# Keys and values turned in 32x32 blocks by VectorE and moved to their rows by DMAs, and another order of the steps of a head

## The chip, the core and the metric

The kernel runs on one core of a Trainium2 chip. A core has five engines with instruction streams of their own: TensorE (PE, matmuls, with the loading of its weights as PEld), VectorE (DVE), ScalarE (ACT), GpSimd (POOL) and SyncE (SP, which here only issues DMAs). Engines wait for each other by semaphores. The metric is the device time of one execution in microseconds (us); lower is better.

## The reference

One inference step of a decoder of two layers: layer 0 mixes tokens by gated linear attention (GLA) with four heads, layer 1 by a gated MLP; each is followed by a dense MLP. There are 256 prompt tokens and 8 x 8 sample tokens, 320 columns in all, and a carried state for each of the 8 sample sequences and 4 heads. The change is in the GLA layer:

```python
def step(s, inp):
    qi, ki, vi, gi = inp
    b = jnp.cumsum(gi, axis=-2)
    b_last = b[..., -1:, :]
    q_dec = qi * jnp.exp(b)
    k_inv = ki * jnp.exp(-b)
    k_to_end = ki * jnp.exp(b_last - b)
    scores = jnp.where(causal, jnp.einsum('bhtk,bhsk->bhts', q_dec, k_inv), 0.0)
    o = (jnp.einsum('bhtk,bhkv->bhtv', q_dec, s)
         + jnp.einsum('bhts,bhsv->bhtv', scores, vi))
    s_new = (jnp.exp(b_last[..., 0, :])[..., None] * s
             + jnp.einsum('bhsk,bhsv->bhkv', k_to_end, vi))
    return s_new, o
...
o = o * lax.rsqrt(jnp.mean(jnp.square(o), axis=-1, keepdims=True) + HEAD_NORM_EPS) * norm_g
o = o.reshape(bsz, t, GLA_VAL_DIM).astype(x.dtype) * jax.nn.silu(r)
return o @ w_out, s_fin.astype(s0.dtype)
```

A head has 256 key columns and 512 value columns; its state is 256 x 512. The last two einsums sum over tokens (s), so they want keys and values with tokens along the partitions, while the projections leave them with features along the partitions.

## The kernel before

**Weight products.** Activations are held as features x 320 tokens. Every weight product is three matmuls of a high and a low part (mm3, lines 161 to 163). A unit is 512 KB of weights: SP loads it into raw (line 138, three buffers), ACT casts it to wh (line 144), DVE subtracts to wl (line 145), and PE runs 24 matmuls on it, into PSUM tiles mm (four banks). The bulk of the kernel is this stream.

**A head.** Each head projects its keys and queries (project_kq), values (project_v) and gates r (project_r), in the order v, kq, r for head 0 and kq, v, r for the others. When a product is done, ev_k, ev_q and ev_v evict it. ev_k makes kend (keys decayed to the end, prompt) and kst (sample keys as high and low parts); PE transposes both (lines 420 and 422, with ident as the other operand) into a PSUM tile gl, from where ACT copies the prompt part to ktp (424) and ACT and DVE in turn copy 32 rows each into kz (429, 431). ev_v copies the prompt values to vfm (447), makes vst, transposes both on PE (456, 458), and copies them to vtp (ACT, 460) and vts (DVE, 461). Over four heads these are 96 transposes of 128x128.

**The steps of a head.** While PE runs the next projection, a Side object puts a head's attention in between, some steps after each unit. The steps are sample_scores, sample_first (loads of states 0 and 1 by SP, line 578, and the first part of the sample output hd.po, line 587), and then sixteen sample steps (sequence b, half kt), with prompt_scores, prompt_o(0), prompt_o(1), prompt_state(0) and prompt_state(1) one after every two of them. A sample step takes the high and low part of the state (ACT sth, line 597; DVE stl, line 598), adds two matmuls to hd.po (line 600), forms the update kz x vts on PE (line 603), and DVE decays and adds it to the state (line 604); after the second half POOL writes the state (line 607). Step (b, 0) loads the state of sequence b + 2. prompt_o multiplies scores and vtp (lines 542, 543; ACT copies and squares, DVE sums), prompt_state ktp and vtp (line 558; ACT copies to S, line 560; POOL writes it, line 562). Last come sample_o (copy, four transposes, sum, square, reduction, a product with ones, and a reciprocal root by ACT and DVE, lines 612 to 625 and 186 to 190), weigh (506) and finish (512).

**What sets the order.** The engines' instruction order is fixed when the program is built: a scheduler places the instructions of the steps and of the weight stream by its own estimate of when they are ready. PSUM tiles gl have four buffers; the tiles with tag st (states, S, and at the start xr) have four too; kz, qm and scst are single. The steps of the last head lie beside the product with w_out (first group mm of its first columns, over four quarters q of its rows, of which the last needs head 3's output). second_half flushes the remaining steps, closes the heads' pools, opens new ones and loads z with POOL.

Of the kernel before, what the change touches and what calls it, by code (L numbers as in the profile page):

```python
# [8 lines left out]
F32 = mybir.dt.float32  # L9
F32R = mybir.dt.float32r  # L10
# [67 lines left out]
def step_kernel(ctx: ExitStack, tc: tile.TileContext, A):  # L78
# [3 lines left out]
    def nm(s):  # L82
        uid[0] += 1
        return f"{s}_{uid[0]}"
# [198 lines left out]
    kz = gp.tile([P, 2, 4, DK], F32R, tag="kz", name="kz")  # L283
# [7 lines left out]
    def load_gates():  # L291

        nc.sync.dma_start(wgr, A["gla_w_low"])
        wgr2 = gp.tile([P, 2, DV], F32, tag="vtp", name="wgr2")[:].rearrange("p a b -> p (a b)")
# [32 lines left out]

    def chunks(ap):
        return ap.rearrange("p (n w) -> p n w", w=CH)

    class Head:
# [6 lines left out]
        def tiles(hd):  # L338
# [59 lines left out]

        def ev_k(hd, kt, ps):
# [17 lines left out]
            pt = gltile()  # L417
            ks = kst[:].rearrange("p b c t -> p (b c t)")
            for blk in range(2):
                nc.tensor.transpose(pt[:, blk * P : (blk + 1) * P], kend[:, blk * P : (blk + 1) * P], ident[:])  # L420
            for g in range(2):
                nc.tensor.transpose(pt[:, TP + g * P : TP + (g + 1) * P], ks[:, g * P : (g + 1) * P], ident[:])
            cs = slice(kt * P, (kt + 1) * P)
            nc.scalar.copy(hd.ktp[:, :, cs], pt[:, 0:TP].rearrange("p (b f) -> p b f", f=P))
            for i in range(4):
                rows = slice(32 * i, 32 * (i + 1))
                src = pt[rows, TP:].rearrange("p (b f) -> p b f", f=P)
                if i % 2:
                    nc.scalar.copy(kz[rows, :, i, cs], src)
                else:  # L430
                    nc.vector.tensor_copy(kz[rows, :, i, cs], src)
# [13 lines left out]
        def ev_v(hd, vt, ps):  # L445
            vfm = g2.tile([P, TP], F32, tag="vfm", name=nm("vfm"))
            nc.scalar.copy(vfm[:], ps[:, 0:TP])
# [5 lines left out]
            pt = gltile()  # L453
            vs = vst[:].rearrange("p b c t -> p (b c t)")
            for blk in range(2):
                nc.tensor.transpose(pt[:, blk * P : (blk + 1) * P], vfm[:, blk * P : (blk + 1) * P], ident[:])  # L456
            for g in range(2):
                nc.tensor.transpose(pt[:, TP + g * P : TP + (g + 1) * P], vs[:, g * P : (g + 1) * P], ident[:])  # L458
            cs = slice(vt * P, (vt + 1) * P)
            nc.scalar.copy(hd.vtp[:, :, cs], pt[:, 0:TP].rearrange("p (b f) -> p b f", f=P))  # L460
            nc.vector.tensor_copy(hd.vts[:, :, cs], pt[:, TP:].rearrange("p (b f) -> p b f", f=P))
# [71 lines left out]
        def prompt_o(hd, i):  # L533
# [19 lines left out]
        def prompt_state(hd, kt):  # L553
# [3 lines left out]
            for blk in range(2):  # L557
                nc.tensor.matmul(pu[:], hd.ktp[:, blk, kt * P : (kt + 1) * P], hd.vtp[:, blk, :],  # L558
                                 start=(blk == 0), stop=(blk == 1))
# [4 lines left out]
        def sample_scores(hd):  # L564
            for g in range(2):
# [14 lines left out]
        def sample_first(hd):  # L580

            hd.st = {}
            hd.load(0)
            hd.load(1)
# [520 lines left out]
```

## Time and profile before

| | us |
|---|---|
| median of three runs (2703.96 to 2704.41) | 2704.05 |
| the profiled execution's own time | 2703.75 |
| its span in the trace | 2702.0 |
| granted TensorE clock, mean | 0.999 |

The page of a profile has the busy time of each engine, the span in 40 slices, and the chain of work that ended last. A group of instructions is a line with its engine and operation, output<-input, the count, the summed busy time, the mean duration of one in ns, and the idle time of the engine just before them with what ended it. Matmuls overlap on PE, so their spacing in a timeline, not their duration, is what they take from it. In a timeline a row is a start, a length (of a run of equal instructions, with their count), and in brackets the idle time before it and what ended that. DMA rows show a queue, a size and the median time from issue to landing. The lines themselves stand in the prediction.

### The profile page before, as it was taken

How to read it: one execution, taken by the hardware profiler on the slowest of the kernel's cores; microseconds unless marked ns; L12 is line 12 of the kernel's file. 1: busy time of each engine (PE TensorE's matmuls, PEld its weight loads, DVE VectorE, ACT ScalarE, POOL GpSimd, SP SyncE). 2: the span in 40 equal slices, each digit the busy share in tenths (PEclk: the TensorE clock that was granted, in tenths of full speed). 3: DMA queues.
4: the chain of work that ended last, by engine and by line, in shares of the span. 5: the costliest groups of instructions: out<-in, count | busy, mean ns of one | idle time of the engine just before them, and what ended most of it. 6: DMA issues, size and time to landing. Idle time of an engine off the chain costs nothing.

```text
span 2702.0 us, 44679 instructions
## 1 busy us (share of the span) xinstructions
PE 2692.4 (100%) x18515; PEld 2669.7 (99%) x18515; DVE 1543.5 (57%) x2289; ACT 1182.8 (44%) x1702; POOL 53.5 (2%) x83
## 2 busy tenths in 40 slices
PE   9999999999999999999999999999999999999998
PEld 9999999999999999999999999999999999999998
DVE  6667577885444444444468775587444444444456
ACT  6545455464234334333445554355334323333434
POOL 1000001000000000000001000000000000000000
PEclk9999999999999999999999999999999999999999
DMA  7656556644445455444445444454444545554442
GB/s 243 193 188 228 185 190 218 211 146 156 152 151 154 151 154 151 153 151 153 150 148 171 150 140 136 140 162 155 150 155 150 154 151 153 152 153 152 153 152 79
DMA packets 126396, 434.53 MB, mean 161 GB/s; under 512 B 13680, under 2 KB 17904, under 8 KB 126192
## 3 DMA queue, kind: packets, MB, share of 16 engines
q1 hardware_dynamic: 119136, 407.82, 48.6%
q0 software_dynamic: 6512, 23.20, 2.6%
q8 instruction: 145, 2.38, 0.4%
q10 hardware_dynamic: 544, 0.66, 0.1%
q14 instruction: 59, 0.48, 0.1%
HBM read 409.60 MB, written 22.02 MB: 160 GB/s over the span
## 4 chain that ended last, share of the span: by engine, by line
PE 99%; ACT 0%; DMA 0%; DVE 0%; issue 0%; ACTq 0%; DVEq 0%
PE mm L161 32%; PE mm L163 31%; PE mm L162 31%; PE gl L600 1%; PE gl L603 1%; PE gl L558 1%; PE gl L948 0%; PE gl L542 0%; DMA raw<-gla_w_in 0%; ACT z L1038 0%; PE gl L943 0%; DMA xr<-xT 0%; PE gl L543 0%; PE gl L458 0%; PE gl L456 0%; PE gl L521 0%
## 5 line engine op out<-in xcount | busy, mean ns | idle before, releaser
L145 DVE TENSOR_TENSOR wl<-raw,wh 128x1024 fp32r<-128x1024 f32 (+1 forms) x740 | 901.6, 1219 | 938.8 <-ACT wh L144 936.3
L144 ACT CAST wh<-raw 128x1024 fp32r<-128x1024 f32 (+1 forms) x740 | 771.3, 1044 | 1201.3 <-PE mm L163 1080.9
L163 PE MATMUL mm<-yh,wh 128*128 128x320 f32 x2624 | 805.0, 307 | 0.0
L161 PE MATMUL mm<-yh,wl 128*128 128x320 f32 x2624 | 803.1, 308 | 0.0
L162 PE MATMUL mm<-yl,wh 128*128 128x320 f32 x2624 | 794.2, 303 | 0.0
L161 PE MATMUL mm<-hh,wl 128*128 128x320 f32 x2048 | 630.8, 308 | 0.0
L163 PE MATMUL mm<-hh,wh 128*128 128x320 f32 x2048 | 628.7, 307 | 0.0
L162 PE MATMUL mm<-hl,wh 128*128 128x320 f32 x2048 | 619.6, 303 | 0.0
L162 PEld LDWEIGHTS mm<-yl,wh 128*128 128x128 f32 x2624 | 492.5, 188 | 0.0
L161 PEld LDWEIGHTS mm<-yh,wl 128*128 128x128 f32 x2624 | 490.9, 188 | 0.0
L163 PEld LDWEIGHTS mm<-yh,wh 128*128 128x128 f32 x2624 | 490.8, 187 | 0.0
L162 PEld LDWEIGHTS mm<-hl,wh 128*128 128x128 f32 x2048 | 384.4, 188 | 0.0
L161 PEld LDWEIGHTS mm<-hh,wl 128*128 128x128 f32 x2048 | 384.4, 188 | 0.0
L163 PEld LDWEIGHTS mm<-hh,wh 128*128 128x128 f32 x2048 | 383.0, 187 | 0.0
L161 PE MATMUL mm<-xh,wl 128*128 128x320 f32 x768 | 241.1, 314 | 0.9 <-DVE wl L145 0.5
L163 PE MATMUL mm<-xh,wh 128*128 128x320 f32 x768 | 236.7, 308 | 0.0
L162 PE MATMUL mm<-xl,wh 128*128 128x320 f32 x768 | 234.7, 306 | 0.0
L161 PEld LDWEIGHTS mm<-xh,wl 128*128 128x128 f32 x768 | 144.1, 188 | 5.4 <-issue 1.9
L162 PEld LDWEIGHTS mm<-xl,wh 128*128 128x128 f32 x768 | 144.3, 188 | 3.5 <-issue 1.2
L163 PEld LDWEIGHTS mm<-xh,wh 128*128 128x128 f32 x768 | 143.9, 187 | 1.3
L857 DVE TENSOR_TENSOR hl<-f,hh 128x320 fp32r<-128x320 f32 x128 | 62.3, 489 | 29.4 <-ACT hh L856 29.4
L161 PE MATMUL mm<-oh,wl 128*128 128x320 f32 x256 | 78.1, 309 | 0.6 <-DVE nw L187 0.6
(268 smaller groups left out, 2112.2 us busy)
## 6 DMA issues: line engine op xcount, KB each, us to landing
raw<-mlp_w SPq DMA_DIRECT2D x512, 512.0 KB, 3.5
raw<-gla_w_in SPq DMA_DIRECT2D x94, 512.0 KB, 4.2
raw<-sg_w_in SPq DMA_DIRECT2D x64, 512.0 KB, 3.5
st<-state SPq DMA_DIRECT2D x32, 512.0 KB, 4.3
o_state_s<-st POOLq DMA_DIRECT2D x32, 512.0 KB, 3.8
raw<-gla_w_out SPq DMA_DIRECT2D x32, 512.0 KB, 4.2
raw<-sg_w_out SPq DMA_DIRECT2D x32, 512.0 KB, 3.5
z<-xT POOLq DMA_DIRECT2D x2, 1280.0 KB, 11.6
```

What stands on the lines that cost most here:

```text
L144: nc.scalar.copy(hi[:, ks, :], raw[:, ks, :])
L145: nc.vector.tensor_sub(lo[:, ks, :], raw[:, ks, :], hi[:, ks, :].bitcast(F32))
L161: nc.tensor.matmul(ps, wl[:, kk, s], x_h, start=first, stop=False)
L162: nc.tensor.matmul(ps, wh[:, kk, s], x_l, start=False, stop=False)
L163: nc.tensor.matmul(ps, wh[:, kk, s], x_h, start=False, stop=last)
L558: nc.tensor.matmul(pu[:], hd.ktp[:, blk, kt * P : (kt + 1) * P], hd.vtp[:, blk, :], start=(blk == 0), stop=(blk == 1))
L600: nc.tensor.matmul(po[:], qm[:, kt, b * P : (b + 1) * P], part[:], start=False, stop=(b == DB - 1 and kt == 1 and part is sth))
L603: nc.tensor.matmul(pu[:], kz[:, g, i, kt * P : (kt + 1) * P], hd.vts[:, g, :], start=True, stop=True)
L857: nc.vector.tensor_sub(hl[:, j, 0:T], f[:], hh[:, j, 0:T].bitcast(F32))
```

## The change

The transposes on PE and the copies behind them are dropped. DVE transposes the same 128x256 pieces in blocks of 32x32 (values straight from PSUM, keys from kend and kst) into a new tile blk, which is taken from the ring of tag st. A block is then turned in itself but stands in the wrong 32 partitions; gather moves the blocks to their rows by four DMAs (one for each source group i) of 32 partitions, with pieces of 128 bytes, for each target group q. Per head there are 32 such DMAs for the keys (POOL) and 32 for the values, of which eight (last half, odd q) go to ACT's queue and the rest to POOL. vtp and vts become one tile va, kz and ktp get another layout, and the readers take views of them. sample_scores and prompt_scores come first, then two empty steps (four in head 3), then sample_first, and the prompt parts stand ahead of sample steps 0, 2, 6 and 8. The loads of states 0 and 1 move into sample_scores.

```diff
--- before.py
+++ after.py
@@ -341,9 +345,18 @@
             hd.kip = gp.tile([P, 2, TP], F32, tag="kip", name=nm("kip"))
             hd.kte = gp.tile([P, 2, T], F32, tag="kte", name=nm("kte"))
             hd.kis = gp.tile([P, 2, DB, 4, DS], F32, tag="kis", name=nm("kis"))
-            hd.ktp = gp.tile([P, 2, DK], F32, tag="ktp", name=nm("ktp"))
-            hd.vtp = gp.tile([P, 2, DV], F32, tag="vtp", name=nm("vtp"))
-            hd.vts = gp.tile([P, 2, DV], F32R, tag="vts", name=nm("vts"))
+
+            hd.ktp = gp.tile([P, 2, 2, P], F32, tag="ktp", name=nm("ktp"))
+            hd.va = gp.tile([P, 2, 2, 2, 2, P], F32, tag="vtp", name=nm("va"))
+
+        def vt_prompt(hd, vt, blk):
+            return hd.va[:, vt // 2, 0, vt % 2, blk, :]
+
+        def v_prompt(hd, blk):
+            return hd.va[:, :, 0, :, blk, :]
+
+        def v_sample(hd, g):
+            return hd.va[:, :, 1, :, g, :].bitcast(F32R)
 
         def gate_logits(hd):
 
@@ -395,6 +408,18 @@
             nc.vector.tensor_copy(fac[:, :, 7:8], d3)
             nc.vector.tensor_mul(fac[:, :, 6:7], d2, d3)
             nc.vector.tensor_mul(fac[:, :, 5:6], fac[:, :, 2:3], d3)
+
+        def blocks(hd):
+
+            return g3.tile([P, 4, TP], F32, tag="st", name=nm("blk"))
+
+        def gather(hd, dst, blk, q, queue):
+
+            n = blk.shape[1] // P
+            src = blk.rearrange("p (n q f) -> p n q f", q=4, f=32)
+            out = dst.rearrange("p (n i f) -> p n i f", i=4, f=32)
+            for i in range(4):
+                queue.dma_start(out[32 * q : 32 * (q + 1), :, i, :], src[32 * i : 32 * (i + 1), :, q, :])
 
         def ev_k(hd, kt, ps):
             ei, ee = hd.ei[kt], hd.ee[kt]
@@ -414,21 +439,16 @@
             hi = kst[:, :, 0:2, :]
             nc.scalar.copy(hi.bitcast(F32R), bc4(kte[:, TP:T]).to_broadcast(two))
             nc.vector.tensor_sub(kst[:, :, 2:4, :], bc4(kte[:, TP:T]).to_broadcast(two), hi)
-            pt = gltile()
-            ks = kst[:].rearrange("p b c t -> p (b c t)")
-            for blk in range(2):
-                nc.tensor.transpose(pt[:, blk * P : (blk + 1) * P], kend[:, blk * P : (blk + 1) * P], ident[:])
-            for g in range(2):
-                nc.tensor.transpose(pt[:, TP + g * P : TP + (g + 1) * P], ks[:, g * P : (g + 1) * P], ident[:])
-            cs = slice(kt * P, (kt + 1) * P)
-            nc.scalar.copy(hd.ktp[:, :, cs], pt[:, 0:TP].rearrange("p (b f) -> p b f", f=P))
-            for i in range(4):
-                rows = slice(32 * i, 32 * (i + 1))
-                src = pt[rows, TP:].rearrange("p (b f) -> p b f", f=P)
-                if i % 2:
-                    nc.scalar.copy(kz[rows, :, i, cs], src)
-                else:
-                    nc.vector.tensor_copy(kz[rows, :, i, cs], src)
+            if kt == 0:
+                hd.kb = hd.blocks()
+            nc.vector.transpose(hd.kb[:, kt, :], kend[:])
+            nc.vector.transpose(hd.kb[:, 2 + kt, :], kst[:].rearrange("p b c t -> p (b c t)"))
+            if kt == 1:
+                kb = hd.kb[:].rearrange("p a b -> p (a b)")
+                for q in range(4):
+                    hd.gather(kz[:, q].bitcast(F32).rearrange("p k b f -> p (k b f)"), kb[:, 2 * TP :], q, nc.gpsimd)
+                for q in range(4):
+                    hd.gather(hd.ktp[:].rearrange("p k b f -> p (k b f)"), kb[:, 0 : 2 * TP], q, nc.gpsimd)
 
         def ev_q(hd, kt, ps):
             qd = hd.qd[:, kt, :]
@@ -443,22 +463,20 @@
             nc.vector.tensor_sub(qv[:, :, DB * DS : DB * DS + DS], qs, qv[:, :, 0:DS].bitcast(F32))
 
         def ev_v(hd, vt, ps):
-            vfm = g2.tile([P, TP], F32, tag="vfm", name=nm("vfm"))
-            nc.scalar.copy(vfm[:], ps[:, 0:TP])
+            if vt % 2 == 0:
+                hd.vb = hd.blocks()
+            nc.vector.transpose(hd.vb[:, vt % 2, :], ps[:, 0:TP])
             vst = g2.tile([P, DB, 4, DS], F32, tag="vst", name=nm("vst"))
             two = [P, DB, 2, DS]
             hi = vst[:, :, 0::2, :]
             nc.scalar.copy(hi.bitcast(F32R), bc4(ps[:, TP:T]).to_broadcast(two))
             nc.vector.tensor_sub(vst[:, :, 1::2, :], bc4(ps[:, TP:T]).to_broadcast(two), hi)
-            pt = gltile()
-            vs = vst[:].rearrange("p b c t -> p (b c t)")
-            for blk in range(2):
-                nc.tensor.transpose(pt[:, blk * P : (blk + 1) * P], vfm[:, blk * P : (blk + 1) * P], ident[:])
-            for g in range(2):
-                nc.tensor.transpose(pt[:, TP + g * P : TP + (g + 1) * P], vs[:, g * P : (g + 1) * P], ident[:])
-            cs = slice(vt * P, (vt + 1) * P)
-            nc.scalar.copy(hd.vtp[:, :, cs], pt[:, 0:TP].rearrange("p (b f) -> p b f", f=P))
-            nc.vector.tensor_copy(hd.vts[:, :, cs], pt[:, TP:].rearrange("p (b f) -> p b f", f=P))
+            nc.vector.transpose(hd.vb[:, 2 + vt % 2, :], vst[:].rearrange("p b c t -> p (b c t)"))
+            if vt % 2:
+                for q in range(4):
+                    hd.gather(hd.va[:, vt // 2].rearrange("p c v b f -> p (c v b f)"),
+                              hd.vb[:].rearrange("p a b -> p (a b)"), q,
+                              nc.scalar if vt == 3 and q % 2 else nc.gpsimd)
 
         def project_kq(hd, side):
 
@@ -538,9 +556,9 @@
             po = gltile()
             pv = po[:].rearrange("p (v t) -> p v t", t=TP)
             for v in range(2):
-                vs = slice((2 * i + v) * P, (2 * i + v + 1) * P)
-                nc.tensor.matmul(pv[:, v, :], hd.vtp[:, 0, vs], scp[:, 0:W0], start=(v == 0), stop=False)
-                nc.tensor.matmul(pv[:, v, P:TP], hd.vtp[:, 1, vs], scp[:, W0:], start=False, stop=(v == 1))
+                vt = 2 * i + v
+                nc.tensor.matmul(pv[:, v, :], hd.vt_prompt(vt, 0), scp[:, 0:W0], start=(v == 0), stop=False)
+                nc.tensor.matmul(pv[:, v, P:TP], hd.vt_prompt(vt, 1), scp[:, W0:], start=False, stop=(v == 1))
             nc.scalar.copy(o_all[:, 4 * h + 2 * i : 4 * h + 2 * i + 2, 0:TP], pv)
             sq = gp.tile([P, 2, TP], F32, tag="sq", name=nm("sq"))
             nc.scalar.activation(sq[:], pv, AF.Square)
@@ -555,13 +573,16 @@
                 hd.S = g3.tile([P, 2, DV], F32, tag="st", name=nm("S"))
             pu = gltile()
             for blk in range(2):
-                nc.tensor.matmul(pu[:], hd.ktp[:, blk, kt * P : (kt + 1) * P], hd.vtp[:, blk, :],
+                nc.tensor.matmul(pairs(pu), hd.ktp[:, kt, blk, :], hd.v_prompt(blk),
                                  start=(blk == 0), stop=(blk == 1))
             nc.scalar.copy(hd.S[:, kt, :], pu[:])
             if kt == 1:
                 nc.gpsimd.dma_start(A["o_state_p"][hd.h].rearrange("(k p) v -> p k v", p=P), hd.S[:])
 
         def sample_scores(hd):
+            hd.st = {}
+            hd.load(0)
+            hd.load(1)
             for g in range(2):
                 pc = gltile(32)
                 for kt in range(2):
@@ -579,12 +600,9 @@
 
         def sample_first(hd):
 
-            hd.st = {}
-            hd.load(0)
-            hd.load(1)
             hd.po = gltile()
             for g in range(2):
-                nc.tensor.matmul(hd.po[:], scst[:, g, :], hd.vts[:, g, :], start=(g == 0), stop=False)
+                nc.tensor.matmul(pairs(hd.po), scst[:, g, :], hd.v_sample(g), start=(g == 0), stop=False)
 
         def sample_step(hd, b, kt):
 
@@ -600,7 +618,7 @@
                 nc.tensor.matmul(po[:], qm[:, kt, b * P : (b + 1) * P], part[:], start=False,
                                  stop=(b == DB - 1 and kt == 1 and part is sth))
             pu = gltile()
-            nc.tensor.matmul(pu[:], kz[:, g, i, kt * P : (kt + 1) * P], hd.vts[:, g, :], start=True, stop=True)
+            nc.tensor.matmul(pairs(pu), kz[:, i, kt, g, :], hd.v_sample(g), start=True, stop=True)
             nc.vector.scalar_tensor_tensor(st[:, kt, :], st[:, kt, :], hd.dec[:, kt, NCH + b : NCH + b + 1],
                                            pu[:], op0=ALU.mult, op1=ALU.add)
             if kt == 1:
@@ -629,14 +647,17 @@
         def steps(hd):
 
             yield hd.sample_scores
+            yield hd.prompt_scores
+            for _ in range(2 if hd.h < H - 1 else 4):
+                yield lambda: None
             yield hd.sample_first
             sample = [lambda b=b, kt=kt: hd.sample_step(b, kt) for b in range(DB) for kt in range(2)]
-            prompt = [hd.prompt_scores, lambda: hd.prompt_o(0), lambda: hd.prompt_o(1),
-                      lambda: hd.prompt_state(0), lambda: hd.prompt_state(1)]
-            for i, p in enumerate(prompt):
-                yield p
-                yield from sample[2 * i : 2 * i + 2]
-            yield from sample[2 * len(prompt) :]
+            prompt = {0: lambda: hd.prompt_o(0), 2: lambda: hd.prompt_o(1),
+                      6: lambda: hd.prompt_state(0), 8: lambda: hd.prompt_state(1)}
+            for i, x in enumerate(sample):
+                if i in prompt:
+                    yield prompt[i]
+                yield x
             yield hd.sample_o
             yield hd.weigh
             yield hd.finish
```

The new order of the instructions is shown at two places. The names are tiles with the number of their buffer's use: st a state, sth and stl its high and low part, va the transposed values, gl and mm PSUM tiles, oh and ol the parts of the heads' output; line numbers are those of the file that the rows belong to.

First place, PE in the sample phase of head 3. Before, a piece of it near prompt_state (L600 the state's part of the output, L603 the update):

```order
L603 MATMUL gl_4555<-vts_3987,kz 128x512
L603 MATMUL gl_4564<-vts_3987,kz 128x512
L161 MATMUL mm_4577<-xh_89,wl_4581 128x320
L600 MATMUL gl_4374<-stl_4550,qm 128x512
L600 MATMUL gl_4374<-sth_4549,qm 128x512
L162 MATMUL mm_4577<-xl_90,wh_4580 128x320
L163 MATMUL mm_4577<-xh_89,wh_4580 128x320
L600 MATMUL gl_4374<-stl_4559,qm 128x512
L600 MATMUL gl_4374<-sth_4558,qm 128x512
L161 MATMUL mm_4577<-xh_89,wl_4581 128x320
```

Now, the start of the sample phase of head 3 on PE (L605 is sample_first, L560 and L561 are prompt_o, L618 and L621 the successors of L600 and L603):

```order
L161 MATMUL mm_4873<-oh_4868,wl_5109 128x320
L162 MATMUL mm_4873<-ol_4869,wh_5108 128x320
L605 MATMUL gl_4540<-va_4052,scst 128x512 x2
L560 MATMUL gl_4544<-scp,va_4052 128x256
L561 MATMUL gl_4544<-scp,va_4052 128x128
L560 MATMUL gl_4544<-scp,va_4052 128x256
L561 MATMUL gl_4544<-scp,va_4052 128x128
L618 MATMUL gl_4540<-stl_4556,qm 128x512
L618 MATMUL gl_4540<-sth_4555,qm 128x512
L621 MATMUL gl_4561<-va_4052,kz 128x512
L618 MATMUL gl_4540<-stl_4595,qm 128x512
L618 MATMUL gl_4540<-sth_4594,qm 128x512
```

And its end (L633 transposes the sample output, L643 is the product with ones):

```order
L618 MATMUL gl_4540<-stl_4932,qm 128x512
L618 MATMUL gl_4540<-sth_4931,qm 128x512
L633 MATMUL gl_4973<-ident,os_4971 128x128 x4
L643 MATMUL gl_4983<-s_694_4543,ones 128x320
L161 MATMUL mm_5246<-oh_4868,wl_5250 128x320
```

Before, weight matmuls stand between any few rows of the sample phase. Now the phase stands together: from L605 to L643 one weight matmul is left, the last of mm_4873; 143 of the products with w_out (mm_4870 to mm_4873, with parts oh and ol of heads 0 to 2) have moved ahead of it, and the next one, mm_5246, reads the weights wl_5250.

Second place, POOL's queue in head 0, ahead of and at the first state writes. Before:

```order
L262 AFFINE_SELECT ms_115<-ms_115 128x32
L262 AFFINE_SELECT ms_119<-ms_119 128x32
L607 DMA o_state_s<-st_926 128x2x512
L607 DMA o_state_s<-st_928 128x2x512
L607 DMA o_state_s<-st_981 128x2x512
L607 DMA o_state_s<-st_1072 128x2x512
```

Now (L422 is a gather, L625 the successor of L607):

```order
L262 AFFINE_SELECT ms_115<-ms_115 128x32
L262 AFFINE_SELECT ms_119<-ms_119 128x32
L422 DMA va_512<-blk_513 32x8x32 x16
L422 DMA va_512<-blk_540 32x8x32 x8
L422 DMA ktp_511<-blk_849 32x4x32 x6
L422 DMA kz<-blk_849 32x4x32 x16
L422 DMA ktp_511<-blk_849 32x4x32 x10
L625 DMA o_state_s<-st_936 128x2x512
```

Ahead of the first state write of head 0 stand 56 gathers where none stood.

More of the change, by code (lines that the diff above doesn't have):

```diff
@@ L280, in step_kernel @@
     nc.vector.memset(fac[:], 1.0)
[L283 removed]
+    kz = gp.tile([P, 4, 2, 2, P], F32R, tag="kz", name="kz")
     nc.gpsimd.memset(kz[:].bitcast(F32), 0.0)
@@ L293, in load_gates @@
         nc.sync.dma_start(wgr, A["gla_w_low"])
-        wgr2 = gp.tile([P, 2, DV], F32, tag="vtp", name="wgr2")[:].rearrange("p a b -> p (a b)")
+        wgr2 = gp.tile([P, 4, DV], F32, tag="vtp", name="wgr2")[:].rearrange("p a b -> p (a b)")[:, 0 : H * DK]
         for i in range(6):
```

2 lines of the change are left out of this document (added).

## The prediction

> **What bounds the kernel now.** I read the page first: its busy times, its chain of waits and the clock row.
>
> ```profile
> span 2702.0 us, 44679 instructions
> PE 2692.4 (100%) x18515; PEld 2669.7 (99%) x18515; DVE 1543.5 (57%) x2289; ACT 1182.8 (44%) x1702; POOL 53.5 (2%) x83
> ...
> PEclk9999999999999999999999999999999999999999
> ...
> PE 99%; ACT 0%; DMA 0%; DVE 0%; issue 0%; ACTq 0%; DVEq 0%
> ```
>
> TensorE (PE) is busy all the span at a full clock, and 99% of the chain that ends last is PE following PE. So two things alone move the time: PE work that goes away, and stretches in which PE has to stand. VectorE (DVE, 57%), ScalarE (ACT) and GpSimd (POOL, 2%) have room on average; what decides is whether they have it where PE waits for them.
>
> **What goes.** The groups of PE instructions by line give the transposes:
>
> ```profile
> L456 PE MATMUL gl<-ident,vfm 128*128 128x128 f32 x32 | 6.2, 271 | 0.0
> L458 PE MATMUL gl<-ident,vst 128*128 128x128 f32 x32 | 6.1, 272 | 0.0
> ...
> L422 PE MATMUL gl<-ident,kst 128*128 128x128 f32 x16 | 3.1, 272 | 0.0
> L420 PE MATMUL gl<-ident,kend 128*128 128x128 f32 x16 | 3.0, 271 | 0.0
> ```
>
> That is 96 instructions and 18.4 us busy. Matmuls overlap, so 18.4 us is an upper bound; the time they take from PE is their spacing, which PE's timeline in head 0 shows:
>
> ```profile
> 41.09 0.38 PE L456 MATMUL gl<-ident,vfm 128*128 128x128 f32 x2
> 41.31 0.38 PE L458 MATMUL gl<-ident,vst 128*128 128x128 f32 x2
> 41.53 0.38 PE L456 MATMUL gl<-ident,vfm 128*128 128x128 f32 x2
> 41.74 0.38 PE L458 MATMUL gl<-ident,vst 128*128 128x128 f32 x2
> 41.88 0.39 PE L161 MATMUL mm<-xh,wl 128*128 128x320 f32 x1
> 42.12 0.31 PE L162 MATMUL mm<-xl,wh 128*128 128x320 f32 x1
> 42.26 0.31 PE L163 MATMUL mm<-xh,wh 128*128 128x320 f32 x1
> ```
>
> Weight matmuls follow each other at 0.14. L162 starts at 42.12, so L161 behind eight transposes held PE from about 41.98: eight took 41.98 - 41.09 = 0.89 us, 0.111 each. 96 x 0.111 = **10.7 us less PE work**. This is also nearly all that can be gained, 0.40%: no other PE instruction leaves.
>
> **What comes on DVE, ACT and POOL.** Per head DVE gets 12 transposes of 128x256 and loses four casts of vts and four of kz; ACT loses fourteen copies.
>
> ```profile
> L447 ACT COPY vfm<-mm 128x256 f32<-128x256 f32 x16 | 6.0, 376 | 10.7 <-PE mm L163 10.7
> L461 DVE CAST vts<-gl 128x256 fp32r<-128x256 f32 x16 | 6.8, 423 | 7.9 <-ACT vtp L460 7.9
> L431 DVE CAST kz<-gl 32x256 fp32r<-32x256 f32 x16 | 6.6, 413 | 0.7 <-ACT ktp L424 0.4
> ```
>
> No row shows a DVE transpose. A pass over 128x256 took 0.42 us here (L461), a two-operand pass over 128x512 0.69; I take 0.42, so 12 x 0.42 - 4 x 0.42 - 4 x 0.41 = 1.7 us more DVE per head, from 0 to 5 by the two rows. That is off PE's path as long as DVE has idle time, and DVE's fullest stretch, the later steps of head 1, has little (columns: PE, weight loads, DVE, ACT, POOL busy with their counts, clock, DMA share, GB/s; the first row is head 3's later steps):
>
> ```profile
> 425.00:452.00 27.00, 27.00 (x165) 24.95 (x164) 21.89 (x34) 15.45 (x29) 4.13 (x6) 1.00 0.71 236
> 240.00:266.00 26.00, 26.00 (x177) 25.35 (x176) 24.71 (x48) 14.15 (x24) 1.45 (x2) 1.00 0.77 274
> ```
>
> 24.7 us of 26 (second row), with PE still busy all of it. The transposes themselves fall into the projections ahead of the steps; I put them at nothing, and keep 0 to 3 us of stalls for heads 0 to 2, of which I take 1, for steps that now run into the next head's projections.
>
> Per head the gathers are 56 DMAs on POOL and 8 on ACT. No row shows one of this kind (32 partitions, 4 or 8 pieces of 128 bytes). POOL's own rows bound the issue:
>
> ```profile
> L607 POOL DMA_DIRECT2D o_state_s<-st x32 | 23.3, 727 | 402.2 <-DVE st L604 391.5 <-DVE fac L393 10.7
> L909 POOL DMA_DIRECT2D bsp<-sg_wT x8 | 4.5, 573 | 2.4 <-DMA bsp<-sg_bs 1.3 <-DMA bsp<-sg_wT 0.8 <-issue 0.2
> ```
>
> From 0.57 (2 KB) to 0.73 (512 KB); I take 0.7, so 56 x 0.7 = 39 us of POOL per head of about 110 us. ACT's eight I take as SyncE (SP) issues a state load:
>
> ```profile
> 411.45 0.43 SPq L578 DMA_DIRECT2D st<-state  x1
> ```
>
> 8 x 0.43 = 3.4 us against the 14 x 0.37 = 5.2 us that its copies leave free. A chain of each head now runs eviction, DVE transpose, gather, landing, and the sample steps stand later in PE's order to make room: in heads 1 and 2 by 165 to 185 rows, about 27 us. By my count of PE's rows the last gather of head 3 lands some 18 us before the first matmul that reads it, of head 0 some 3 us before.
>
> [...] POOL's issues fall amid DVE work: in the first window row above six take 4.13 us, 0.69 each, while DVE is busy 21.89 of 27 us. [...]
>
> **What moves: head 3.** Before, the 16 sample steps of head 3 stand one by one among weight matmuls, up to the last L600 (the rows below show it near 451), and PE is busy 27.00 of 27.00 us in the window above. In the new order 143 weight matmuls of w_out's first three quarters (mm_770 to mm_773) stand ahead of them, and then sample_first, both prompt_o, all 16 steps, both prompt_state and sample_o stand together with one weight matmul among them. The next weight matmul (mm_819) needs wl_823; ACT's two casts for it stand behind the head's rsqrt, and DVE's subtraction behind weigh (L506). So PE runs into head 3's own chain of DVE, ACT and state DMAs uncovered. Its work there, by the spacing of starts in the timeline:
>
> ```profile
> 450.42 0.39 PE L600 MATMUL gl<-stl,qm 128*128 128x512 f32 x1
> 450.65 0.39 PE L600 MATMUL gl<-sth,qm 128*128 128x512 f32 x1
> ...
> 425.77 1.88 PE L558 MATMUL gl<-vtp,ktp 128*128 128x512 f32 x4
> ```
>
> 50 matmuls of the kinds L600, L603 and L587 at 0.23 are 11.5 us; eight L558 instructions at 0.43 (four start and end within 1.88, the last overlapping) 3.4; L542/L543, the transposes L615 and L625 together 3.6 by the same reading: **18.5 us**.
>
> The chain, with T0 where PE comes to sample_first (about 435 us by row count). DVE's steps, back to back in the timeline:
>
> ```profile
> 405.97 0.75 DVE L604 SCALAR_TENSOR_TENSOR st<-st,dec,gl 128x512 f32<-128x512 f32 x1
> 406.63 0.69 DVE L598 TENSOR_TENSOR stl<-st,sth 128x512 fp32r<-128x512 f32 x1
> 407.23 0.74 DVE L604 SCALAR_TENSOR_TENSOR st<-st,dec,gl 128x512 f32<-128x512 f32 x1
> ```
>
> An update (L604) holds DVE 0.66 us and a low part (L598) 0.60, so a state of two steps costs 2.5. Only four tiles of the state ring exist, so states 4 to 7 wait for the write of an earlier state (or of S) and then for their load. The median landings:
>
> ```profile
> st<-state SPq DMA_DIRECT2D x32, 512.0 KB, 4.3
> o_state_s<-st POOLq DMA_DIRECT2D x32, 512.0 KB, 3.8
> ...
> o_state_p<-S POOLq DMA_DIRECT2D x4, 512.0 KB, 5.7
> ```
>
> State 0 is done at T0 + 4; its write and the load of state 4 into its tile take 3.8 + 4.3 and some 0.3 between: state 4 is there at 12.4, when states 1 to 3 are just done. States 5 and 6 follow states 2 and 3, at 18 to 21, and state 7 follows S and state 1 at 21 to 23. The last L600 is then at T0 + 24.5 (24 to 26). The bound from DVE alone, 14 x 0.60 + 14 x 0.66 + 1 for prompt_o's sums = 18.7 (the three sums are passes over 128x256), gives 20.
>
> Then comes sample_o, whose ACT durations the timeline of before shows:
>
> ```profile
> 451.84 0.59 ACT L612 COPY os<-gl 128x512 f32<-128x512 f32 x1 [2.77 <-PE gl L600]
> ...
> 455.76 0.37 ACT L618 COPY o_all<-gl 128x256 f32<-128x256 f32 x1 [2.23 <-PE gl L615]
> 456.62 0.42 ACT L621 ACTIVATE sq<-o_all 128x256 f32<-128x256 f32 x1 [0.49 <-DVE o_all L619]
> ...
> 461.98 1.28 ACT L186 ACT_TABLE_LOAD   x1
> 463.28 0.53 ACT L186 ACTIVATE ny<-gl,eps_h 128x320 f32<-128x320 f32 x1
> 464.82 1.05 ACT L144 CAST wh<-raw 128x1024 fp32r<-128x1024 f32 x1 [1.01 <-DMA raw<-gla_w_out]
> ```
>
> From the last L600: 0.4 to the copy os, 0.6, four transposes 0.6, 0.4, DVE's sum 0.4, the square 0.4, DVE's reduction 0.6 and L625 with its waits 0.7, by 28.8; the table load starts behind the square and ends by 29.3; ny 0.5; two casts 2.1; DVE's second wl 1.2 and hand-overs 0.4: PE goes on at **T0 + 33.5**. It stands 33.5 - 18.5 = **15 us**, from 10 (states loaded in time) to 20 (landings as slow as o_state_p's). What follows is covered: z's load lands 11.6 us after its issue, beside 144 weight matmuls (21 us).
>
> ```profile
> z<-xT POOLq DMA_DIRECT2D x2, 1280.0 KB, 11.6
> ```
>
> **The sum.** On the profiled execution, 2703.75 us (a span of 2702.0 and 1.75 around it; 0.30 under the median of 2704.05): 2703.75 - 10.7 + 15 + 1 = 2709.1, and on the median's scale 2709.4, nearly the bound of what counts as slower. I give **2710**. The forecast's own range is -10.7 + 10 to -10.7 + 20 + 3, that is 2703 to 2716.
>
> **Rivals.** (1) *Hidden after all*: the stretch of head 3 costs PE under 5 us and the removed transposes count. The time is 2704.05 - 10.7 + 0 to 5 = 2693 to 2698. For it: PE has no wait over 1 us anywhere before. Against it: DVE's work alone in that stretch, 18.7 us, is more than PE's 18.5, and sample_o, rsqrt and the casts lie behind it. Chance 0.10.
>
> (2) *Slower, by the chain of state tiles*: write and load in turn take longer once four loads stand one after another on SP without a raw load between, and every late state is on PE's path. If each of the two rounds costs 5 us more than the medians, PE stands 25 us: 2704 - 10.7 + 25 + 1 = 2719. It decides from about 2 us more per round. For it: state loads had other landings' company before (DMA share 0.71 in the window above). Against it: PE stands, so the weights' traffic stops as well. Chance 0.17.
>
> (3) *Slower, by the gathers*: POOL needs more than 0.7 us per DMA. Head 3 has 18 us for about 40 of them, so this decides from 0.7 + 18/40 = 1.15 us; at 1.5 PE waits some 14 us more in head 3 and about as much in each of heads 1 and 2, together 42: 2752. The row against it is the 0.73 for 512 KB; for it is that no row shows such small pieces and that in the new order each gather of POOL waits for the one eight before it, so that a landing of over 8 x 1.15 = 9 us would do it (2 KB pieces of L909 landed in 5.4). Chance 0.08.
>
> ```profile
> bsp<-sg_wT POOLq DMA_DIRECT2D x8, 2.0 KB, 5.4
> ```
>
> [...]
>
> (4) *The change does not do what it says* (transposes left in place) is excluded: the new order of PE has none of the 96 rows.
>
> **How the numbers follow.** The forecast has 0.65, the rivals 0.10, 0.17 and 0.08. A measurement of this kernel can tell about 0.2% from no change, 5.4 us: faster is below 2698.6, slower above 2709.5. The forecast's 0.65 lies about evenly on both sides of 2709.5: 0.33 slower and 0.32 the same; rivals 2 and 3 are slower, rival 1 faster or at its edge. So faster 0.10, same 0.32, slower 0.58. The range leaves out rival 1's lower part and rival 3: 2697 to 2722.
>
> **What will show it.** Right: no L456, L458, L420, L422 among PE's groups, and PE's busy time less by some 10 us; in the timeline of head 3 a stretch of about 33 us from 435 with PE idle near 15, ended by DVE (L604's and L598's successors), by state loads, and at its end by DVE wl; POOL's gathers at 0.6 to 0.75. Wrong: PE waits on gathers in heads 0 to 2, or gaps of over 3 us there; a gather issue over 1 us; a stretch in head 3 under 25 us or over 40.

## The result and the profile after

| | us |
|---|---|
| before, median of 5 runs (2703.96 to 2704.41) | 2704.13 |
| changed, median of 5 runs (2725.42 to 2731.30) | 2729.40 |
| ratio | 1.0091, 95% interval 1.0076 to 1.0106 |
| the changed kernel's profiled execution, its span | 2729.40, 2727.6 |

The change makes the kernel 25 us slower. The sign was forecast, the size not: 2710, with 2697 to 2722 as the range. The page of the changed kernel (PE, the clock of 40 slices, the chain of waits):

```profile
span 2727.6 us, 44891 instructions
...
PE 2697.5 (99%) x18419; PEld 2667.4 (98%) x18419; DVE 1548.2 (57%) x2305; ACT 1172.6 (43%) x1652; POOL 177.9 (7%) x307
...
PEclk9999999899999999999999999999999999999999
...
PE 94%; ACT 2%; DMA 2%; issue 1%; DVE 1%; POOL 0%; ACTq 0%; POOLq 0%; DVEq 0%
```

PE has 96 instructions less, and yet its busy time grew by 5 us: the clock row has one of the 40 slices at 8 tenths, and a busy time at a lower clock is no measure of work (the four transposes of the sample output are 1.12 us long at a clock of 0.50, 0.60 at 1.00 before). PE's share of the chain fell from 99% to 94%. What PE waited for in the first 500 us (engine, line, what ended the wait: total us, times, longest):

```profile
PE mm L161 <- DVE wl L145: 5.7, 3, 4.3
PE gl L621 <- ACT S L578: 5.5, 2, 2.9
PE gl L618 <- DVE stl L616: 4.9, 5, 2.4
PE gl L643 <- DVE s L640: 2.1, 1, 2.1
PE gl L621 <- DVE st L622: 1.8, 1, 1.8
```

No wait is ended by a gather. The gathers themselves, by line (count, busy, mean ns, idle time of POOL ahead of them), and DVE's transposes:

```profile
L422 POOL DMA_DIRECT2D va<-blk x96 | 55.4, 584 | 41.8 <-DVE blk L474 29.5 <-DMA va<-blk 5.7 <-DVE scs L592 3.4
L422 POOL DMA_DIRECT2D kz<-blk x64 | 34.8, 552 | 20.0 <-PE gl L618 6.5 <-PE mm L163 5.6 <-issue 5.1
...
L468 DVE STREAM_TRANSPOSE blk<-mm 128x256 f32<-128x256 f32 x16 | 6.8, 433 | 0.7 <-PE mm L163 0.6
```

To see where the time went I took the start-to-start distance of PE's matmuls, less the usual distance of their line (0.146 for L161, 0.23 for the 512-wide ones, and so on; all of the trace's matmul starts), and added it up. It counts waits and slow clock together:

| lost by PE, us | before | changed |
|---|---|---|
| 0 to 400 us (heads 0 to 2) | 6.1 | 18.9 |
| 400 to 500 us (head 3) | 1.7 | 24.0 |
| after 500 us | 3.8 | 3.9 |

So 12.8 us more in heads 0 to 2, 22.3 in head 3, nothing later; with 10.7 us less work this makes 24.4 of the 25.6 us between the two profiled executions. The rest stays open.

**Head 3.** Its phase begins at T0 = 449.41 and ends with the next weight matmul at 488.37, 39.0 us, in which PE has 18.5 us of work at full clock. Marks of the chain, in the timelines of PE and of ACT:

```profile
449.41 0.63 PE L605 MATMUL gl<-va,scst 128*128 128x512 f32 x2
...
478.11 0.63 PE L618 MATMUL gl<-sth,qm 128*128 128x512 f32 x1
479.41 1.12 PE L633 MATMUL gl<-ident,os 128*128 128x128 f32 x4 [0.68 <-ACT os L630]
482.62 1.41 PE L643 MATMUL gl<-s,ones 128*128 128x320 f32 x2 [2.09 <-DVE s L640]
...
488.37 0.63 PE L161 MATMUL mm<-oh,wl 128*128 128x320 f32 x1 [4.35 <-DVE wl L145]
```

```profile
461.95 0.62 ACT L615 CAST sth<-st 128x512 fp32r<-128x512 f32 x1 [0.51 <-DMA st<-state]
...
467.98 1.14 ACT L615 CAST sth<-st 128x512 fp32r<-128x512 f32 x2 [3.36 <-DMA st<-state]
472.61 1.14 ACT L615 CAST sth<-st 128x512 fp32r<-128x512 f32 x2 [3.49 <-DMA st<-state]
```

State 4 is there at T0 + 12.5, state 5 at 18.6, state 6 at 23.2; each time ACT waited for the load. The last L618 starts at T0 + 28.7, and weights go on at T0 + 39.0. And the clock (the window columns of the prediction: PE, weight loads, DVE, ACT, POOL busy, clock, DMA share, GB/s):

```profile
458.00:466.00 8.00, 7.17 (x23) 3.71 (x21) 6.52 (x11) 3.45 (x6) 2.14 (x3) 1.00 0.87 267
466.00:478.00 12.00, 7.46 (x17) 4.04 (x16) 7.56 (x12) 3.51 (x6) 2.14 (x3) 0.66 0.75 276
478.00:488.00 10.00, 3.26 (x8) 1.23 (x7) 6.99 (x13) 6.01 (x8) 0.71 (x1) 0.50 0.27 86
488.00:494.00 6.00, 5.63 (x22) 5.63 (x23) 5.48 (x10) 2.32 (x4) 1.80 (x2) 0.53 0.81 260
```

From 470 PE runs at half speed (a clock of 0.50, weight matmuls 0.27 apart instead of 0.146), and for 5 us more after it has weights again: 22 matmuls in 488 to 494 that would take 3.2 us. The late loads were all issued before the clock fell. In the rows below, the first has SP's four state loads, the last of them issued at 469.19; the second is the landing of the load of state 6 (issued at 466.27); then come two windows with the columns above:

```profile
457.35 12.21 SPq L599 DMA_DIRECT2D st<-state  x4
...
DMA to landing us min/median/max: 6.2/6.2/6.2
...
468.00:470.00 2.00, 0.63 (x2) 0.32 (x3) 1.37 (x3) 1.11 (x2) 0.00 (x0) 0.95 0.97 333
470.00:472.00 2.00, 2.00 (x5) 1.05 (x4) 1.24 (x2) 0.00 (x0) 0.46 (x1) 0.50 0.98 336
```

**Heads 0 to 2.** The largest wait there, in head 1, in the timelines of ACT, DVE and PE:

```profile
242.09 1.28 ACT L382 ACT_TABLE_LOAD   x1
...
243.87 1.28 ACT L396 ACT_TABLE_LOAD   x1
...
245.90 0.57 ACT L578 COPY S<-gl 128x512 f32<-128x512 f32 x1
...
246.52 0.51 PE L621 MATMUL gl<-va,kz 128*128 128x512 f32 x1 [2.85 <-ACT S L578]
```

L621 needs a PSUM tile of gl, of which there are four; the one it waits for is freed by ACT's copy to S, and this stands in ACT's queue behind two table loads and the exponentials of the next head's gates (L382, L396). Before, head 1's phase was some 27 us earlier, and its last copy to S (here L560) was done 5.5 us ahead of the first table load of the next head's gates (here L360):

```profile
220.45 0.59 ACT L560 COPY S<-gl 128x512 f32<-128x512 f32 x1 [0.35 <-PE gl L558]
...
226.55 1.28 ACT L360 ACT_TABLE_LOAD   x1
```

In the changed kernel, the clock behind this wait is 0.58 in 248 to 252; around the 1.8 us in head 0 it stayed at 1.00 (first row below):

```profile
120.00:140.00 20.00, 18.16 (x109) 16.44 (x108) 15.70 (x34) 16.98 (x26) 2.86 (x4) 1.00 0.63 208
...
248.00:252.00 4.00, 4.00 (x19) 4.00 (x18) 4.00 (x14) 3.02 (x7) 0.71 (x1) 0.58 0.78 254
```

### The profile page after: what moved, and what is told of

Same layout as the page of the kernel before. It is cut to its first block, busy times and chain, and to the rows that moved or that the text cites. A ratio compares the mean times of both kernels' runs of the same rounds, so it can differ in the third digit from the quotient of the medians.

```text
span 2727.6 us, 44891 instructions
## 1 busy us (share of the span) xinstructions
PE 2697.5 (99%) x18419; PEld 2667.4 (98%) x18419; DVE 1548.2 (57%) x2305; ACT 1172.6 (43%) x1652; POOL 177.9 (7%) x307
## 4 chain that ended last, share of the span: by engine, by line
PE 94%; ACT 2%; DMA 2%; issue 1%; DVE 1%; POOL 0%; ACTq 0%; POOLq 0%; DVEq 0%
PE mm L161 31%; PE mm L163 30%; PE mm L162 30%; PE gl L618 1%; DMA va<-blk 0%; PE gl L621 0%; DMA ktp<-blk 0%; ACT L373 0%; ACT L382 0%; PE gl L576 0%; PE gl L969 0%; DVE wl L145 0%; ACT wh L144 0%; DMA st<-state 0%; DMA raw<-gla_w_in 0%
## 5 line engine op out<-in xcount | busy, mean ns | idle before, releaser
L161 PE MATMUL mm<-yh,wl 128*128 128x320 f32 x2624 | 803.1, 308 | 0.0
L161 PE MATMUL mm<-hh,wl 128*128 128x320 f32 x2048 | 630.8, 308 | 0.0
L161 PEld LDWEIGHTS mm<-yh,wl 128*128 128x128 f32 x2624 | 491.0, 188 | 0.0
L161 PEld LDWEIGHTS mm<-hh,wl 128*128 128x128 f32 x2048 | 384.4, 188 | 0.0
L161 PE MATMUL mm<-xh,wl 128*128 128x320 f32 x768 | 239.3, 312 | 1.8 <-DVE wl L145 1.3
L161 PEld LDWEIGHTS mm<-xh,wl 128*128 128x128 f32 x768 | 145.6, 190 | 5.5 <-DVE wl L145 1.9
L161 PE MATMUL mm<-oh,wl 128*128 128x320 f32 x256 | 79.1, 313 | 5.2 <-DVE wl L145 4.3
L163 PE MATMUL mm<-oh,wh 128*128 128x320 f32 x256 | 79.5, 311 | 0.0
```

The lines of the kernel that those rows point to most:

```text
L161: nc.tensor.matmul(ps, wl[:, kk, s], x_h, start=first, stop=False)
L163: nc.tensor.matmul(ps, wh[:, kk, s], x_h, start=False, stop=last)
```

## The experiments

All ratios are to the kernel before on the same chip. Theory A at the outset: the gathers, by the time the scheduler allots to them, place the sample phases late, into bare stretches and into the next head's gates. The scheduler's estimate itself is on no record; that part of A is an assumption. Rivals: the new order of the steps does it; the gathers' traffic does it; PE's own work does it.

**1. The order of the steps alone** (order_only). In the kernel before; the loads of states 0 and 1 move into sample_scores as well:

```diff
             yield hd.sample_scores
+            yield hd.prompt_scores
+            for _ in range(2 if hd.h < H - 1 else 4):
+                yield lambda: None
             yield hd.sample_first
...
+            prompt = {0: lambda: hd.prompt_o(0), 2: lambda: hd.prompt_o(1),
+                      6: lambda: hd.prompt_state(0), 8: lambda: hd.prompt_state(1)}
```

> The kernel before, with only the new order of a head's steps (transposes stay on PE). Theory A (the gathers, by the time the scheduler allots to them, are what moves the sample phases behind the weight matmuls; the order of the steps does not): PE's order has 264 weight matmuls inside head 3's sample phase, as before (262), so the time is that of before, 2704, within 3 us, with no wait of PE over 1.5 us. Rival B (the new order of the steps itself makes the phases late and bare): the loss of the change without its 10.7 us of gain, so 2729 + 11 = 2740.

Measured 2712.03, ratio 1.0027 (1.0015 to 1.0039): between the two. PE's timeline shows where:

```profile
462.65 0.31 PE L163 MATMUL mm<-oh,wh 128*128 128x320 f32 x1
464.66 0.81 PE L625 MATMUL gl<-s,ones 128*128 128x320 f32 x2 [1.70 <-DVE s L622]
470.63 0.64 PE L161 MATMUL mm<-oh,wl 128*128 128x320 f32 x1 [5.17 <-DVE wl L145]
```

Nothing is lost up to 400 us (6.3, before 6.1), but 8 us in head 3: its phase is covered, but ends so late that the weight matmuls run out ahead of sample_o's reduction and the rsqrt. I then suspected the empty steps.

**2. The order without the empty steps** (order_no_empty): in experiment 1, `range(0)` for the count of empty steps.

> The kernel before with the new order of the steps, but without the empty steps. Theory A (the 8 us that the order alone cost come from the four empty steps of head 3: they delay its end past the last covering weight matmuls, so that PE waits for the rsqrt and the next weights): the waits of 1.9 and 5.5 us at 463 and 465 us go, 2704, within 1.5. Rival B (the places of prompt_scores and the prompt parts cost it): 2712.

Measured 2704.80, ratio 1.0002 (0.9993 to 1.0011). The empty steps cost the 8 us (by the place of the loss, the four of head 3); the order of the other steps costs nothing.

**3. Head 3 with transposes on PE** (h3_pe). In the changed kernel, ev_k and ev_v of head 3 take their old body:

```diff
+            if hd.h < 3:
+                return hd.ev_v_gather(vt, ps)
+            vfm = g2.tile([P, TP], F32, tag="vfm", name=nm("vfm"))
...
+                nc.tensor.transpose(pt[:, blk * P : (blk + 1) * P], vfm[:, blk * P : (blk + 1) * P], ident[:])
```

> The changed kernel, with head 3's keys and values turned by PE and copied as before (24 transposes back; head 3's prompt values are rounded to fp32r on the way, which changes the output a little). Theory A (a ledger of the changed trace: head 3's bare phase costs 22.8 us, heads 0 to 2 about 14): 2729 - 22.8 + 2.7 = 2709, with the waits of heads 0 to 2 unchanged. Rival B (the gathers cost by their traffic or their issue wherever they run, of which a quarter goes): about 2722.

Measured 2716.94, ratio 1.0049 (1.0033 to 1.0066), 12.5 us less than the change. The time lies between A's 2709 and B's 2722 and decides nothing by itself. By the sum of distances head 3 loses 10.2 us (24.0 with gathers), and its waits are again those of experiment 1 (L161 after L678: longest 5.3). So taking the gathers from head 3 brings back 13.8 us, less 2.7 for its transposes; A's 22.8 had left out that the empty steps then come into force. The waits of heads 0 to 2 stand unchanged, as A said. But what follows the second wait on S, in head 2, differs: head 2 loses 4.0 us instead of 6.5. The first row below has the waits on S of this run, then come the wait in head 2 and a window behind it (PE busy, clock, DMA share, GB/s), first of this run, then of the change:

```profile
PE gl L656 <- ACT S L613: 5.5, 2, 2.9
...
361.33 0.50 PE L656 MATMUL gl<-va,kz 128*128 128x512 f32 x1 [2.69 <-ACT S L613]
362.00:364.00 2.00, 2.00 (x15) 1.00 0.59 223
...
361.48 0.79 PE L621 MATMUL gl<-va,kz 128*128 128x512 f32 x1 [2.68 <-ACT S L578]
362.00:364.00 2.00, 2.00 (x9) 0.50 0.51 193
```

Behind a wait of nearly the same length the clock was 1.00 here and 0.50 there.

**4. The gathers with the old order** (gather_only): in the changed kernel, the steps in the order of before; the loads of states 0 and 1 stay in sample_scores.

> The changed kernel with the old order of the steps (sample_first and its loads right after sample_scores, no empty steps). Theory A: the gathers still push the phases behind the weight matmuls; head 2 gets a bare stretch too (127 weight matmuls inside its phase where the changed kernel has 274, head 3 34 where it has 1), so it is no better: 2730 to 2750. Rival B (the order of the steps makes the loss): near 2704 - 10.7 = 2693.

Measured 2729.70, ratio 1.0095 (1.0080 to 1.0110), as slow as the change. The losses move (head 2 loses 14.0 instead of 6.5, head 1 3.2 instead of 5.0) and the sum nearly stays. The order of the steps is not what makes the change slow.

**5. Four more matmuls per step in head 3** (filler4):

```diff
+            for _ in range(4 if hd.h == H - 1 else 0):
+                nc.tensor.matmul(pairs(pu), scst[:, g, :], hd.v_sample(g), start=True, stop=True)
             nc.tensor.matmul(pairs(pu), kz[:, i, kt, g, :], hd.v_sample(g), start=True, stop=True)
```

> The changed kernel with four more matmuls ahead of each update of head 3 (64 x 0.23 = 14.8 us of PE work whose result is overwritten). Theory A (head 3's phase is set by DVE, ACT and the state DMAs, and PE idles there for about 17 us, part of it at half clock): the phase grows by less than 5 us, and may even shrink where the clock stays up: 2725 to 2734. Rival B (PE's own work sets the phase): 2729 + 15 = 2744.

Measured 2733.27, ratio 1.0108 (1.0093 to 1.0123): by the medians 3.9 us for 14.8 us of added work. The four executions lie at 2730.5 and 2730.8 (mean clock 0.997) and at 2735.8 and 2736.5 (0.994 and 0.995), so the price is 1 to 7 us. In the profiled one, 2730.8, the phase lasts 42.8 us instead of 39.0, and the filled stretch keeps its clock until sample_o:

```profile
460.00:470.00 10.00, 10.00 (x39) 6.98 (x38) 5.62 (x9) 3.50 (x7) 2.21 (x4) 1.00 0.71 237
470.00:480.00 10.00, 9.67 (x41) 7.15 (x39) 7.63 (x12) 2.98 (x6) 1.98 (x3) 1.00 0.76 268
```

So PE's own work does not set the phase of the change.

**6. The rest of the steps ahead of the next head's gates** (steps_first): `Side(side.steps + gates, ...)` for `Side(gates + side.steps, ...)`.

> The changed kernel with the remaining steps of a head put ahead of the next head's gates in the program (the changed kernel has gates first). Theory A (the waits at 127, 243 and 358 us come from ACT's and DVE's gate work of the next head standing ahead of S and of the state update): those waits, with the half clock behind them some 11 us, go; but the phases of heads 1 and 2 get dense (104 weight matmuls inside instead of 297), so new waits on the state DMAs may appear: 2718 to 2732. Rival B (they come from the gathers): the waits stay at their places, 2729.

Measured 2774.12, ratio 1.0261 (1.0245 to 1.0276), far outside. The waits on S are gone, and a worse one has come, three times 11 us, since the queries' eviction needs the gates:

```profile
PE mm L161 <- DVE qd L455: 32.5, 3, 11.1
```

This says that gates and steps compete, but not that the gates caused the old waits. The opposite move can.

**7. The next head's gates ahead of a head's steps** (gates_early). In the changed kernel:

```diff
-            hd.project_kq(Side(gates + side.steps, 2 * NU))
+            hd.project_kq(Side(side.steps, 2 * NU))
...
-        side = Side(hd.steps(), 2 * NU + (2 * NU if h < H - 1 else 2))
+        early = [nxt.gate_logits, nxt.gate_sums, nxt.gate_decays] if nxt else []
+        side = Side(early + list(hd.steps()), 2 * NU + (2 * NU if h < H - 1 else 2))
```

> The changed kernel with the gates of the next head put into the program ahead of a head's steps, instead of ahead of what is left of them in the next projection. Theory A (the waits at 127, 243 and 358 us come from the next head's gate work on ACT and DVE, which the later phases of heads 0 to 2 run into): these waits go, about 11 us with the half clock behind them, and head 3's bare phase stays (47 weight matmuls inside, from 1), 2716 to 2722. Rival B (they come from the gathers or the state DMAs): 2727 to 2731.

Measured 2714.61, ratio 1.0036 (1.0023 to 1.0050): 14.8 us less than the change, more than expected. The loss up to 400 us falls from 18.9 to 6.2, that of before; head 3 still loses 23.6, and its longest wait is on the states (5.7). With gathers in every head as in the change, heads 0 to 2 lose no more than before, though head 1's phase still starts at 212.9 (215.6 in the change, 186.7 before). Their cost was the meeting with the gates.

**8. The same without the empty steps** (gates_no_empty):

> gates_early without the empty steps. Theory A (in the changed kernel the gathers, not the empty steps, set where head 3's phase stands; PE's order has 47 weight matmuls inside it with or without them): 2714.6, within 2. Rival B (the empty steps cost their 8 us here too, as they did with the transposes on PE): 2706 to 2708.

Measured 2715.29, ratio 1.0041 (1.0027 to 1.0055). With gathers the empty steps are without effect; the gathers alone place head 3's phase. By which part of theirs is not shown: besides the time that the scheduler allots to them, their tiles blk take places in the ring of the states, and no run separates the two.

**9 to 12. Versions that keep what is free.** Keys gathered in all heads, values transposed by PE, no empty steps (k_all):

> Keys turned by DVE and gathered in all heads, values transposed by PE as before; new order of the steps without empty steps. 32 of 96 transposes go. Theory A (what costs is that the value gathers, which end last before the sample phase, push it; the key gathers have the value projection ahead of it): PE's order has 278 weight matmuls inside head 3's phase, so 2704 - 32 x 0.111 = 2700.5, from 2699 to 2702. Rival B (any gather costs more than its transpose): 2704 or more.

Measured 2701.46, ratio 0.9991 (0.9982 to 1.0000). Head 0's values gathered as well (k_v0):

> As k_all, and head 0's values gathered too (they come first there, ahead of the keys, so their gathers have time). 48 transposes go. Theory A: 2704 - 48 x 0.111 = 2698.8, from 2697 to 2701; head 0's phase starts no later than before by PE's order. Rival B (head 0's gathers of keys and values are too many in a row and its first sample steps wait): over 2701.

Measured 2701.68, ratio 0.9992 (0.9983 to 1.0000), nothing more: A missed. By the sum of distances PE loses some 3 us more in heads 0 to 2 than in k_all; what makes it lose them no run shows. k_all with the gates early (k_all_g):

> k_all with the next head's gates ahead of a head's steps. Theory A (k_all's 1 us short of its 3.6 us are small waits beside the gates in heads 0 to 2): 2700 to 2701.5. Rival B (no effect, or the gates now collide with the evictions): 2701.5 to 2704.

Measured 2701.45, ratio 0.9990 (0.9981 to 0.9998), the edge of A's range but no faster than k_all: no effect. Where the phases are early, as in k_all, the gates are not in their way (2701.45 against 2701.46). Last, gathers everywhere but for head 3's values, with gates early and no empty steps (k_v3_g; heads 0 to 2 keep their values in two tiles of half the columns, and head 3 has vtp and vts):

```diff
+            if hd.h < 3:
+                return hd.ev_v_gather(vt, ps)
...
+                for a in range(2):
+                    rhs = hd.va[a][:, c, :, blk, :]
+                    o = out.rearrange("p (a v f) -> p a v f", a=2, v=2)[:, a]
+                    nc.tensor.matmul(o, lhs, rhs.bitcast(F32R) if c else rhs, start=start and a == 0, stop=stop and a == 1)
```

> Keys gathered in all heads, values gathered in heads 0 to 2 and transposed by PE in head 3, no empty steps, next head's gates ahead of a head's steps. 80 transposes go. Theory A: 80 x 0.111 = 8.9 us gained, some 3 us of small waits in heads 0 to 2: 2695 to 2700. Rival B (the values' gathers in heads 1 and 2 push the phases into waits as in the changed kernel): 2702 to 2708.

Measured **2695.41** (2695.27 to 2695.94), ratio 0.9967 (0.9954 to 0.9979): faster than the kernel before by 8.8 us, of the 8.9 that 80 transposes are worth. Against experiment 8 it differs in head 3's values and in the two tiles; no run parts these, nor shows whether it needs the gates early. Its largest waits of PE:

```profile
PE mm L161 <- DVE wl L145: 1.3, 2, 0.8
PE gl L152 <- DVE ones L116: 1.1, 1, 1.1
PE gl L367 <- DMA kz<-blk: 0.5, 1, 0.5
```

## Why the prediction was right in sign and wrong in size

- **96 transposes, 10.7 us:** right. No run isolates it in the changed kernel, but k_v3_g turns 80 of them into 8.8 us.
- **DVE's transposes at 0.42, 1.7 us per head, off PE's path:** right; 0.43 measured.
- **ACT's eight gathers at 0.43, 3.4 us:** wrong, 0.63 each and 5.3 us in head 3, about what its dropped copies leave free; no wait of PE ends on them.
- **POOL's gathers at 0.7, from 0.57 to 0.73:** right enough, 0.55 to 0.58 in the means over 224 issues; the third rival (over 1.15) fell.
- **Head 3's last gather some 18 us ahead of its reader:** nearly right, 15.3. It is issued at 428.53 and lands 5.6 us later (rows below), at 434.1, and the reader starts at 449.41. PE does not wait for the data; the fixed order has put the reader there. That the scheduler takes gathers to be slower than they are would explain it; no run shows its estimate.

```profile
428.53 0.58 POOL L422 DMA_DIRECT2D va<-blk  x1 [0.69 <-DMA va<-blk]
...
DMA to landing us min/median/max: 5.6/5.6/5.6
```

- **Heads 0 to 2, "0 to 3 us of stalls", taken as 1:** this term failed, 12.8 us. I had read the row of head 1 (DVE 24.7 of 26 us busy) as a matter of DVE's load. What counts is the order in ACT's and DVE's queues: steps that are 27 us later stand behind the next head's gates, with table loads of 1.28 each, and hold PE's PSUM tiles meanwhile (its waits there: 1.78, 2.85 and 2.68). Experiment 7 shows it; experiment 3 shows that head 3 has no part in it. With 1 us here the time would have been 2717.6, inside the range.
- **Head 3, "PE goes on at T0 + 33.5", 15 us, from 10 to 20:** right mechanism, wrong size. T0 + 39.0 and 22.3 us more lost than before. (T0 itself came at 449.4, not at the counted 435, mostly by what heads 0 to 2 had lost.) The parts: state 4 came on time (12.5 against 12.4), state 6 only at 23.2 where I had 21, and the last L618 at 28.7 instead of 24.5; the tail from there took 10.3 instead of 9.0, with L633 at 1.12 (before 0.60) and L643 at 1.41 (0.70). The terms of that tail were also added up wrongly: as listed they end L625 at 28.6, not 28.8, and the table load at 28.6, not 29.3, which would have put PE's return at T0 + 32.8. 2.4 us follow after the phase, and 1.0 goes at 427 us, where a weight matmul waits for ACT's oh. The second rival (5 us more per round of state DMAs) was nearer in time, 2719, but the rounds were less late than that. Of the 4.2 us by which the last L618 came late, 2.2 are there when state 6 arrives, whose load was issued before the clock fell and took 6.2 us to land, not the assumed 4.3: these are the state DMAs. The other 2.0 arise behind it, at a clock of 0.50; how much of them is the clock, and how much state 7, which landed only at T0 + 24.8, no run separates.
- **What no step had:** I priced a wait at its own length. Both failed terms contain half-speed matmuls, in head 3 and for 3.4 and 5.9 us after the waits of 2.85 and 2.68 us in heads 1 and 2. It is not certain to happen: in experiment 3 the clock behind the wait of 2.69 us in head 2 was 1.00.
- **"0 to 5 us" for the hidden case:** the first rival fell. But experiments 7 and 12 show that most of what it hoped for can be had when the gates are moved and head 3's values are left on PE.

## What to carry to other kernels

Work taken from the bounding engine is worth its spacing only if the order of that engine stays covered: look for stretches of its new order without bulk work, and price them by the chains of the other engines (here k_v3_g kept 8.8 of 8.9 us, and the change lost 25). When a phase moves later, check in every engine's queue what it moves into, not how busy the engine is on average. A replacement with a long latency (the gathers of POOL landed 3.3 to 4.5 us after their issue, by the medians) belongs where other work already lies between producer and consumer; the one place without (here the last head's values) can keep the old way.

## What the runs showed of the hardware

A wait of PE can cost more than its length. After the 2.85 us at 243 the mean granted clock of 248 to 252 was 0.58, though PE was busy all of it; in head 3 it fell to 0.50 at 470 and stayed there through many short waits until 5 us after the weights went on at 488; after the 1.78 us at 127 it stayed at 1.00. Length alone did not decide here: the wait at 358 to 361, 2.68 us in the change and 2.69 in h3_pe, was followed by a clock of 0.50 in the one and of 1.00 in the other (experiment 3). In the clock record of the changed kernel's trace the three stretches at 0.50 that end before the kernel does last 3.41, 6.83 and 23.89 us (from 247.9, 360.6 and 469.8); the waits of PE next to their starts, of 2.85, 2.68 and 2.42 us, end at 246.5, 361.5 and 469.4.

The time of one and the same kernel goes with this: the five executions of the change took 2725.42, 2727.82, 2729.40, 2729.99 and 2731.30 us at mean clocks of 0.995, 0.994, 0.993, 0.993 and 0.992. And with useless matmuls put into the waits of head 3 the clock was 1.00 up to sample_o in the profiled execution of filler4 (experiment 5), where the change has 0.66 in 466 to 478. But the mean clock was 0.994 and 0.995 in two of its other three executions; at which place it fell there no trace shows.
